# Rotated q and k from SBUF to SBUF by eight transfers of 32 rows, and the transposes of results placed behind the other transposes

## The chip, the core and the metric

The kernel runs on one core of a Trainium2 chip. The metric is the device time of one execution in microseconds (us). Five engines work side by side, each through its own instructions in order: TensorE (PE, with its weight loads as PEld), VectorE (DVE), ScalarE (ACT), GpSimd (POOL) and SyncE (SP), which here issues nearly all DMA transfers. TensorE writes to PSUM alone; the other engines read its results there.

## What is computed

The reference is one block of a network on a sequence of 1024 tokens with 1024 features. The normed input is projected to twelve segments. One branch is an mLSTM in both directions; the other is a differential attention with 8 heads, and the change lies in it. For each head and each of two half heads j (64 features each), q and k are rotated by their positions, and two softmaxes are subtracted:

```python
dq = apply_rope(b_q.reshape(B, S, DA_HEADS, 2, DA_QK_DIM), positions)
dk = apply_rope(b_k.reshape(B, S, DA_HEADS, 2, DA_QK_DIM), positions)
scores = einsum('bqhjd,bkhjd->bhjqk', qb, k) * scale
p = softmax(scores)
att = einsum('bhqk,bkhd->bqhd', p[:, :, 0] - lam * p[:, :, 1], v)
att = rmsnorm(att, da_subln_g) * (1.0 - lambda_init)
y_b = att * silu(b_z)
```

Both branches are gated, projected, summed, added to the input and normed. All of it is float32 outside; inside, TensorE multiplies each float32 operand as a high part and a low part (H and L), in three products.

## The kernel before, in words

The work comes in three stages: projections with the convolution and the gates (to about 410 us of the profile), the attention (410 to 1130 us), and the mLSTM with the three last projections. All instructions of TensorE stand in an order that a planner writes before the build: `Weaver` puts units of work one after another by assumed costs (MM, TP) and assumed delays (the table LAG), and `weave` interleaves two lists, here `main` (the attention's own units) and `nxt` (projections for the next head, and filling work). From the second stage on only TensorE is held to the written order; the order on DVE, ACT and POOL is chosen by the build's scheduler, and each engine then keeps it.

For each of 8 heads h there are 8 tiles of 128 queries, t = 0 to 7. `da_cycle` (L1008 to L1026) lists the units of one cycle (h, t):

- S: `scores`, 12 matmuls S<-kst,qq (L924). They fill two PSUM tiles, one for each half head. Then DVE takes the row maxima (nm, L927, two), ACT the exponentials (e, L929, two), and DVE the reciprocal, a scaling and the difference of both (L933, L934, L935). The result is p of this t.
- T: `transposes`, four transposes of p of t-1 into a PSUM tile (T<-ident,e, L131), two units a cycle. Each tile is then read by ACT (pH, L948) and by DVE (pL, L949).
- PV: `pv`, two units of 12 matmuls (L960), in odd t. They share one PSUM tile, which ACT copies to att (L962).
- M: `squares`, in even t: two transposes of att into a PSUM tile (T<-ident,att, L131), which ACT squares in two steps (L972) and sums for the norm. I call a cycle with M an even cycle.
- G: `scale`, in t = 4 and 5: four transposes of the norm's factors (T<-ident,rb_y) and a DVE multiply (zg, L992).

T, PV, M and G all take their PSUM tile from the tag "T", which has two buffers in turn. So a unit's tile is free when the tile but one before it has been read. In between lie the pieces of the list `nxt`: one piece is an eighth of a projection to 128 features and 512 tokens, three matmuls of 512 columns (pj<-hH,wH and so on, L429), or, for v, six matmuls of 256 columns (L451).

`da_proj` projects q and k of the next head in two halves of 512 tokens. A projection yields its rows in the order (q or k, half head, feature), with both halves of the rotation in two PSUM tiles. `first` and `second` rotate: DVE multiplies (m, L852 and L853, and hl, L863 and L864), POOL combines (m, L865 and L866), ACT rounds to the high part (hl, L868), POOL makes the low part (hl, L869). The tile hl has one buffer. Then `second` has to bring rows from hl to qq and kst, where rotation halves stand below each other. It does so through a DRAM tile stk: four stores (L873) and two loads (L875), all on SP's queue.

Of the kernel before, what the change touches and what calls it, by code (L numbers as in the profile page):

```python
# [7 lines left out]
F32 = mybir.dt.float32  # L8
# [101 lines left out]
class Block:  # L110
# [731 lines left out]
    def da_proj(self, h, st):  # L842
        A, v, a, p, q = self.A, self.v, self.a, self.p, self.q
        w1 = self.w1
        fb = lambda x: x.bitcast(F32)
        kA, kB = ("rope", h, 0), ("rope", h, 1)

        def first(half, pa):
            c = slice(half * 512, (half + 1) * 512)
            m = [w1.tile([128, 512], F32, name=f"m{i}", tag=f"m{i}", bufs=1) for i in range(2)]  # L850
            st["m"] = m
            v.tensor_tensor(out=m[0], in0=pa, in1=self.cosT[:, c], op=ALU.mult)  # L852
            v.tensor_tensor(out=m[1], in0=pa, in1=self.sinT[:, c], op=ALU.mult)  # L853

        def second(half, pb):
            c = slice(half * 512, (half + 1) * 512)
            if half == 0:
                st["k"] = w1.tile([128, 2, S], F32R, name="kst", tag="kst", bufs=2)
            qq = st["q", half] = w1.tile([128, 2, 512], F32R, name="qq", tag="qq", bufs=3)
            m = st["m"]  # L860

            hl = w1.tile([128, 4, 512], F32R, name="hl", tag="hl", bufs=1)
            v.tensor_tensor(out=fb(hl[:, 2]), in0=pb, in1=self.sinT[:, c], op=ALU.mult)  # L863
            v.tensor_tensor(out=fb(hl[:, 3]), in0=pb, in1=self.cosT[:, c], op=ALU.mult)  # L864
            p.tensor_tensor(out=m[0], in0=m[0], in1=fb(hl[:, 2]), op=ALU.subtract)  # L865
            p.tensor_tensor(out=m[1], in0=fb(hl[:, 3]), in1=m[1], op=ALU.add)  # L866
            for i in range(2):
                a.copy(hl[:, i, :], m[i])  # L868
                p.tensor_tensor(out=hl[:, 2 + i, :], in0=m[i], in1=fb(hl[:, i, :]), op=ALU.subtract)  # L869
            dr = self.dram.tile([2, 4, 2, 32, 512], F32, name="stk", tag="stk", bufs=2)  # L870
            for y in range(2):
                for x in range(2):
                    q.dma_start(out=dr[y, :, x], in_=fb(hl[:, 2 * y + x]))  # L873
            for i, x in enumerate((qq, st["k"][:, :, c])):
                q.dma_start(out=fb(x), in_=dr[:, 2 * i:2 * i + 2].rearrange("y j x i s -> (j x i) y s"))  # L875

        kz = ("w_in", OFF["bz"] + 128 * h)

        def zz(half, ps):
            st["g", half] = g = w1.tile([128, 512], F32, name="zg", tag="zg", bufs=2)  # L880
            a.activation(out=g, in_=ps, func=AF.Tanh, scale=0.5)
            v.scalar_tensor_tensor(out=g, in0=g, scalar=1.0, in1=ps, op0=ALU.add, op1=ALU.mult)

        qk = []
        for half in range(2):
            qk += self.proj(kA, half, lambda ps, half=half: first(half, ps))
            qk += self.proj(kB, half, lambda ps, half=half: second(half, ps), name=("qk", h))
        z = self.proj(kz, 0, lambda ps: zz(0, ps)) + self.proj(kz, 1, lambda ps: zz(1, ps), name=("z", h))
        for half in range(2):
            z[(half + 1) * self.PIECES - 1].after = ((("G", h - 1, half), LAG["G"]),)  # L890
        return qk, z
# [114 lines left out]
    @staticmethod  # L1006
    def da_cycle(cur, prev, t):

        before = cur if t > 0 else prev
        un = []  # L1010
        if cur:
            un.append(cur["S"](t))
        own = cur if t >= 4 else prev
        if own and t % 2 == 0:
            un.append(own["M"]((t // 2 - 2) % 4))
        if prev and t in (4, 5):
            un.append(prev["G"](t - 4))
        own = cur if t >= 3 else prev
        pair = ((t - 1) // 2 - 1) % 4
        if own and t % 2 == 1:  # L1020
            un += [own["PV"](pair, 0), own["PV"](pair, 1)]
        if before:
            un.append(before["T"]((t - 1) % 8, 0))
        if before:
            un.append(before["T"]((t - 1) % 8, 1))
        return un  # L1026


# [613 lines left out]
```

## Time and profile before

| | us |
|---|---|
| median of 3 runs | 1722.02 (1720.14 to 1725.31) |
| the profiled execution | 1722.36 |
| its span, first to last instruction | 1720.5 |
| PE busy, PEld busy | 1660.1, 1392.5 |
| DVE, ACT, POOL busy | 988.8, 777.5, 605.6 |
| mean granted TensorE clock | 0.991 |

The span is 1.9 us shorter than the profiled execution's own time; the rest lies around the instructions. PE is busy in 96% of the span, so time is to be had only from its gaps and from stretches at a lower granted clock, and each new gap on PE counts in full. [...]

### The profile page before, as it was taken

What the parts mean: (1) busy time and instruction counts of PE and PEld (TensorE: products, weight loads), DVE (VectorE), ACT (ScalarE), POOL (GpSimd) and SP (SyncE); (2) the same over time, 40 slices, a digit from 0 to 9 for tenths busy, and PEclk for the clock granted to TensorE, in tenths of its full rate; (3) what the DMA queues carried; (4) which work ended last, traced back from release to release, by engine and by line L of the source; (5) the groups of instructions that cost most, each with busy time, mean ns of one, the idle gap of its engine ahead of it and who ended that gap; (6) DMA issues with size and microseconds to landing.
All of it is one profiled execution on the core that took longest, in us unless ns stands there. A gap on an engine that the chain in (4) does not pass through costs nothing. (4 is left out here: it accounts for less than half of the span.)

```text
span 1720.5 us, 25270 instructions
## 1 busy us (share of the span) xinstructions
PE 1660.1 (96%) x9431; PEld 1392.5 (81%) x9431; DVE 988.8 (57%) x1799; ACT 777.5 (45%) x1554; POOL 605.6 (35%) x680
## 2 busy tenths in 40 slices
PE   7999999999999999999999999999999989999998
PEld 5777887887878987798788878889999867888887
DVE  5778678773376665666566655325666643235533
ACT  7455555552355544454445444324655644122221
POOL 4767666664243233323241322222321311222000
PEclk9999999999999999999999999999999999999999
DMA  5343434344322314131422131155455327344222
GB/s 182 94 130 119 137 121 135 111 129 138 113 98 74 111 38 147 62 98 30 131 84 77 45 122 62 62 178 163 139 169 154 96 79 258 123 147 135 86 87 85
DMA packets 182540, 195.55 MB, mean 114 GB/s; under 512 B 10905, under 2 KB 134130, under 8 KB 182418
## 3 DMA queue, kind: packets, MB, share of 16 engines
q1 hardware_dynamic: 181506, 192.35, 35.8%
q8 instruction: 74, 1.21, 0.3%
q10 hardware_dynamic: 912, 1.59, 0.2%
q14 instruction: 48, 0.39, 0.1%
HBM read 130.89 MB, written 63.01 MB: 113 GB/s over the span
## 5 line engine op out<-in xcount | busy, mean ns | idle before, releaser
L429 PE MATMUL pj<-hH,wH 128*128 128x512 f32 x640 | 269.1, 420 | 3.8 <-DVE hl L864 1.9
L429 PE MATMUL pj<-hH,wL 128*128 128x512 f32 x640 | 253.7, 396 | 1.8 <-POOL wL L207 1.8
L429 PE MATMUL pj<-hL,wH 128*128 128x512 f32 x640 | 253.0, 395 | 0.2 <-DVE hL L580 0.2
L209 POOL TENSOR_TENSOR wL<-raw,wH 128x1024 fp32r<-128x1024 f32 x41 | 99.5, 2426 | 287.4 <-ACT wH L204 284.9
L929 ACT ACTIVATE e<-S,nm 128x1024 f32<-128x1024 f32 x128 | 142.5, 1115 | 104.7 <-DVE nm L927 104.6
L927 DVE TENSOR_REDUCE nm<-S 128x1 f32<-128x1024 f32 x128 | 150.4, 1217 | 16.7 <-PE S L924 15.9
L429 PEld LDWEIGHTS pj<-hH,wH 128*128 128x128 f32 x640 | 122.2, 191 | 39.2 <-issue 15.4
L949 DVE TENSOR_TENSOR pL<-T,pH 128x512 fp32r<-128x512 f32 x128 | 87.9, 688 | 108.7 <-ACT pH L948 107.8
L451 PE MATMUL pj<-wH,hH 128*128 128x256 f32 x512 | 149.8, 293 | 0.3
L429 PEld LDWEIGHTS pj<-hH,wL 128*128 128x128 f32 x640 | 121.9, 190 | 30.8 <-POOL wL L207 3.3
L451 PE MATMUL pj<-wL,hH 128*128 128x256 f32 x512 | 144.8, 283 | 1.4 <-POOL wL L207 1.4
L451 PE MATMUL pj<-wH,hL 128*128 128x256 f32 x512 | 144.5, 282 | 0.0
L429 PEld LDWEIGHTS pj<-hL,wH 128*128 128x128 f32 x640 | 122.6, 192 | 18.7 <-DVE hL L580 0.6
L429 PE MATMUL pj<-sl_yb,wH 128*128 128x512 f32 x384 | 121.8, 397 | 4.3 <-ACT sl_yb L1315 2.4
L924 PE MATMUL S<-kst,qq 64*128 64x512 f32 x768 | 108.8, 413 | 8.0 <-DMA kst<-stk 8.0
L948 ACT CAST pH<-T 128x512 fp32r<-128x512 f32 x128 | 74.9, 585 | 88.0 <-PE T L131 87.5
L204 ACT CAST wH<-raw 128x1024 fp32r<-128x1024 f32 x56 | 58.8, 1051 | 114.0 <-PE pj L429 88.3
L451 PEld LDWEIGHTS pj<-wH,hH 128*128 128x128 f32 x512 | 97.8, 191 | 5.1 <-issue 2.2
L451 PEld LDWEIGHTS pj<-wL,hH 128*128 128x128 f32 x512 | 97.5, 190 | 2.3 <-POOL wL L207 2.3
L451 PEld LDWEIGHTS pj<-wH,hL 128*128 128x128 f32 x512 | 97.7, 191 | 0.1
L924 PEld LDWEIGHTS S<-kst,qq 64*128 64x128 f32 x768 | 68.3, 186 | 35.4 <-issue 10.5
L429 PEld LDWEIGHTS pj<-sl_yb,wH 128*128 128x128 f32 x384 | 73.4, 191 | 22.3 <-DVE sl_yb L1316 3.4
(358 smaller groups left out, 4107.0 us busy)
## 6 DMA issues: line engine op xcount, KB each, us to landing
raw<-in_w_in_dram SPq DMA_DIRECT2D x88, 512.0 KB
stk<-hl SPq DMA_DIRECT2D x64, 256.0 KB
qq<-stk SPq DMA_DIRECT2D x16, 512.0 KB
kst<-stk SPq DMA_DIRECT2D x16, 512.0 KB
x<-in_x_dram SPq DMA_DIRECT2D x8, 512.0 KB
cak<-y SPq DMA_DIRECT2D x16, 256.0 KB
cakH<-cin SPq DMA_DIRECT2D x16, 256.0 KB
cakL<-tz SPq DMA_DIRECT2D x16, 256.0 KB
```

The source lines that it names most:

```text
L204: self.a.copy(wH, raw)
L209: self.p.tensor_tensor(out=wL, in0=raw, in1=wHf, op=ALU.subtract)
L429: self.t.matmul(ps, lhsT=l[:, k, :], rhs=r, start=(n == 0), stop=(n == 23))
L451: self.t.matmul(ps[:, i, :], lhsT=l, rhs=r[:, k, :], start=(kh == 0 and k == 0 and m == 0), stop=(kh == 1 and k == 3 and m == 2))
L924: self.t.matmul(ps[:, o], lhsT=qq[r, x, c], rhs=k[r, y, o], start=(m == 0), stop=(m == 2))
L927: v.tensor_reduce(out=nm, in_=ps, axis=AX.X, op=ALU.max, negate=True)
L929: a.activation(out=e, in_=ps, func=AF.Exp, bias=nm[:, 0:1], accum_out=Z[:, j, t:t + 1])
L948: a.copy(pH[:, :, s], ps)
L949: v.tensor_tensor(out=pL[:, :, s], in0=ps, in1=pH[:, :, s].bitcast(F32), op=ALU.subtract)
```

## The change

Two things are changed. The rows go from hl to kst and qq directly, by eight transfers of 32 partitions each (32 rows, high and low part, 512 tokens: 128 KB), with the rotation half x = 0 first. And in `da_cycle` the unit M, which stood right behind S, stands behind both T units.

```diff
-            dr = self.dram.tile([2, 4, 2, 32, 512], F32, name="stk", tag="stk", bufs=2)
-            for y in range(2):
-                for x in range(2):
-                    q.dma_start(out=dr[y, :, x], in_=fb(hl[:, 2 * y + x]))
-            for i, x in enumerate((qq, st["k"][:, :, c])):
-                q.dma_start(out=fb(x), in_=dr[:, 2 * i:2 * i + 2].rearrange("y j x i s -> (j x i) y s"))
+            for x in range(2):
+                for i, to in enumerate((st["k"][:, :, c], qq)):
+                    for j in range(2):
+                        r, g = 64 * j + 32 * x, 64 * (1 - i) + 32 * j
+                        q.dma_start(out=fb(to[r:r + 32]), in_=fb(hl[g:g + 32, x::2]))
...
             un.append(cur["S"](t))
-        own = cur if t >= 4 else prev
-        if own and t % 2 == 0:
-            un.append(own["M"]((t // 2 - 2) % 4))
         if prev and t in (4, 5):
             un.append(prev["G"](t - 4))
...
             un.append(before["T"]((t - 1) % 8, 1))
+        own = cur if t >= 4 else prev
+        if own and t % 2 == 0:
+            un.append(own["M"]((t // 2 - 2) % 4))
         return un
```

The second edit goes through the planner, so the order of PE is the thing to see. This is PE in the cycle of head 2, t = 6, before, from the end of the first three pieces that follow S on. The names: T_6270 is the tile of M, T_6275 and T_6297 are those of the two T units, S_6304 is the next S.

```order
L131 MATMUL T_6270<-ident_146,att_5626 128x128 x2
L131 MATMUL T_6275<-ident_146,e0_6130 128x128 x4
L429 MATMUL pj_6231<-hH0_170,wH_5832 128x512
L429 MATMUL pj_6231<-hL0_172,wH_5832 128x512
L429 MATMUL pj_6231<-hH0_170,wL_5833 128x512
...
L131 MATMUL T_6297<-ident_146,e0_6130 128x128 x4
L924 MATMUL S_6304<-kst_4924,qq_5133 128x512
```

The same place on PE after the change; again three pieces stand between S and the first row. T_6278 and T_6288 are now the tiles of the two T units, T_6301 is that of M.

```order
L131 MATMUL T_6278<-ident_146,e0_6109 128x128 x4
L429 MATMUL pj_6239<-hH0_170,wH_5838 128x512
L429 MATMUL pj_6239<-hL0_172,wH_5838 128x512
L429 MATMUL pj_6239<-hH0_170,wL_5839 128x512
L131 MATMUL T_6288<-ident_146,e0_6109 128x128 x4
...
L131 MATMUL T_6301<-ident_146,att_5632 128x128 x2
...
L923 MATMUL S_6312<-kst_4928,qq_5138 128x512
```

M has moved from the first place to the last: T, one piece, T, two pieces, M, one piece, next S. Of the two buffers, T_6278 has one, T_6288 the other, and M's tile T_6301 takes that of T_6278. Before, it was the second T that took the buffer of M.

DVE after the change, in the same cycle, from the row maxima of this S (S_6243 and S_6244, the two half heads) on:

```order
L926 TENSOR_REDUCE nm_6257<-S_6243 128x1
L926 TENSOR_REDUCE nm_6261<-S_6244 128x1
L932 RECIPROCAL r_6265<-Z_5630 128x1
L933 TENSOR_SCALAR r_6265<-r_6265,Z_5630,nlam_703 128x1
L934 SCALAR_TENSOR_TENSOR e0_6259<-e1_6263,r_6265,e0_6259 128x1024
L948 TENSOR_TENSOR pL_6193<-T_6278,pH_6192 128x4x128
L948 TENSOR_TENSOR pL_6223<-T_6288,pH_6222 128x4x128
```

ACT after the change, in the same cycle:

```order
L928 ACTIVATE e0_6259,Z_5630<-S_6243,nm_6257 128x1024
L928 ACTIVATE e1_6263,Z_5630<-S_6244,nm_6261 128x1024
L947 CAST pH_6192<-T_6278 128x4x128
L947 CAST pH_6222<-T_6288 128x4x128
L971 ACTIVATE T_6301,ms_5631<-T_6301 128x128 x2
```

On DVE and ACT the reads of the two T tiles stand behind the whole softmax of the S that was issued just before them. Before, ACT had the order e0, e1, first square, pH, second square, and DVE had the five softmax rows and then the first pL, as now; but no unit of that cycle waited for that pL.

## Prediction

> **What bounds the kernel now.** I read the page's busy times first:
>
> ```profile
> span 1720.5 us, 25270 instructions
> PE 1660.1 (96%) x9431; PEld 1392.5 (81%) x9431; DVE 988.8 (57%) x1799; ACT 777.5 (45%) x1554; POOL 605.6 (35%) x680
> ```
>
> PE is the bound; DVE and ACT have slack on average. So I asked next what PE waits for in the attention (410 to 1130 us), where the change lies:
>
> ```profile
> PE S L924 <- DMA kst<-stk: 8.0, 3, 2.7
> PE T L131 <- ACT T L972: 5.6, 6, 1.4
> PE pj L429 <- DVE hl L864: 1.9, 1, 1.9
> PE T L131 <- DVE pL L949: 0.3, 1, 0.3
> ```
>
> These four rows (total, times, longest) are all of PE's gaps in the stage, 15.8 us. A wait can cost more than its gap: in four stretches, each beside one of these gaps, the granted clock stood at half. The table by windows (PE busy first, PEclk third from the end):
>
> ```profile
> 428.05:431.46 3.41, 3.41 (x10) 2.64 (x9) 0.00 (x0) 0.51 (x1) 3.41 (x3) 0.50 1.06 383
> 684.05:690.88 6.83, 6.41 (x18) 4.62 (x19) 3.32 (x5) 2.56 (x5) 0.00 (x0) 0.50 0.29 77
> 851.30:854.71 3.41, 3.41 (x8) 2.67 (x9) 2.36 (x2) 2.13 (x3) 0.00 (x0) 0.50 0.47 139
> 1015.14:1018.55 3.41, 3.39 (x10) 2.32 (x11) 1.71 (x2) 0.45 (x1) 0.00 (x0) 0.50 0.57 154
> ```
>
> The hl wait of 1.9 us and the three kst waits (8.0 in three, the longest 2.7) were each followed by this; the ACT waits, up to 1.4 us, were not. A stretch at half costs half of itself: 1.7, 3.4, 1.7 and 1.7, together 8.5 us.
>
> **The change part by part.** *The transfers.* In the second half of head 2, SP's timeline and the S that waited for it read:
>
> ```profile
> 664.66 4.04 SPq L873 DMA_DIRECT2D stk<-hl  x4
> 668.74 2.22 SPq L171 DMA_DIRECT2D raw<-in_w_in_dram  x1
> 679.36 0.37 SPq L875 DMA_DIRECT2D qq<-stk  x1
> 679.78 0.61 SPq L875 DMA_DIRECT2D kst<-stk  x1
> ```
>
> ```profile
> 684.47 1.65 PE L924 MATMUL S<-kst,qq 64*128 64x512 f32 x6 [2.74 <-DMA kst<-stk]
> ```
>
> The stores are issued by 668.70, the loads wait for them until 679.36 (10.7 us), and S goes on at 684.47, 4.7 us after the last load's issue: 15.8 us in two passes. The new way is one pass, and the trace has no such transfer. Bounds: 4.7 us as the loads, 10.7 us as the stores. Both stay under 15.8 - 2.7 = 13.1 us, so the three kst waits go: -8.0 us, and their clock, -6.8 us. I take some 7 us between the ends, and the sum doesn't depend on it. SP issues 128 transfers in place of 96; at the 0.4 to 1.0 us apiece of these rows that is at most 2 us more a half, and in exchange this goes from its queue:
>
> ```profile
> SPq L875 <- DMA stk<-hl: 148.8, 37, 9.2
> ```
>
> Queued behind that wait stand weight loads (raw). No wait of PE on weights stands among its waits in the stage, so their coming earlier is worth nothing. The earlier release of hl removes the 1.9 us wait at 427 us (there DVE could write hl only after the stores had landed) and its half clock, -1.7. Nothing else in the stage waited on these, so nothing is late next on this path.
>
> *M behind the T units.* The six ACT waits of 5.6 us are a second T that waits for the squares of M, whose tile it inherits. That pair is gone: -5.6 us. Removed in all: 8.0 + 5.6 + 1.9 + 8.5 = **24.0 us**.
>
> What replaces it: M now inherits the tile of the first T, and DVE's last read of that tile (pL) stands behind the whole softmax of the S just issued. So I need two times from the start of S: when PE comes to M, and when that pL ends. First PE, from an even cycle without a wait (head 2, t = 2), which has the same pieces in the old order:
>
> ```profile
> 620.32 1.66 PE L924 MATMUL S<-kst,qq 64*128 64x512 f32 x12
> ...
> 624.06 0.38 PE L131 MATMUL T<-ident,att 128*128 128x128 f32 x2
> 624.28 0.60 PE L131 MATMUL T<-ident,e 128*128 128x128 f32 x4
> 624.63 0.48 PE L429 MATMUL pj<-hH,wH 128*128 128x512 f32 x1
> ...
> 627.46 0.60 PE L131 MATMUL T<-ident,e 128*128 128x128 f32 x4
> 627.99 1.65 PE L924 MATMUL S<-kst,qq 64*128 64x512 f32 x12
> ```
>
> S and three pieces take 3.74 us, a T 0.35, four pieces 2.83, which is 0.70 to 0.75 for one and 1.45 for two. The new order (S, three pieces, T, one, T, two, M) brings PE to M at 3.74 + 0.35 + 0.75 + 0.35 + 1.45 = **6.64 us**. Then the softmax after the S at 627.99, on DVE and on ACT (the ACT row at 623.71 belongs to the S at 620.32):
>
> ```profile
> 628.71 0.69 DVE L949 TENSOR_TENSOR pL<-T,pH 128x512 fp32r<-128x512 f32 x1 [0.18 <-ACT pH L948]
> 629.68 2.35 DVE L927 TENSOR_REDUCE nm<-S 128x1 f32<-128x1024 f32 x2 [0.28 <-PE S L924]
> 633.81 1.28 DVE L935 SCALAR_TENSOR_TENSOR e<-e,r,e 128x1024 f32<-128x1024 f32 x1
> ```
>
> ```profile
> 623.71 1.12 ACT L929 ACTIVATE e<-S,nm 128x1024 f32<-128x1024 f32 x1 [1.89 <-DVE nm L927]
> 630.94 1.12 ACT L929 ACTIVATE e<-S,nm 128x1024 f32<-128x1024 f32 x1 [2.26 <-DVE nm L927]
> ```
>
> The first exponential starts 2.95 us after S, the difference ends 4.15 us later (635.09), pL takes 0.69: the tile is free 4.85 us after the first exponential, 7.80 us after S. PE is there at 6.64: a new wait of **1.16 us in an undisturbed even cycle**. At 623.71 the exponential came 3.39 us after S, which makes it 1.60.
>
> A test of this arithmetic on the old order (head 2, t = 6):
>
> ```profile
> 660.71 1.66 PE L924 MATMUL S<-kst,qq 64*128 64x512 f32 x12
> 669.16 0.66 PE L131 MATMUL T<-ident,e 128*128 128x128 f32 x4 [1.12 <-ACT T L972]
> ```
>
> ```profile
> 665.77 1.11 ACT L929 ACTIVATE e<-S,nm 128x1024 f32<-128x1024 f32 x1
> 668.91 0.19 ACT L972 ACTIVATION_READ_ACCUMULATOR T<-T 128x1 f32 x1
> ```
>
> There PE would come to the second T 627.46 - 620.32 = 7.14 us after S, at 667.85; the squares ended at 669.10, and T started at 669.16: 1.3 us late, and the profile shows a gap of 1.12. It also shows why: the exponential came 5.06 us after S, since on ACT the roundings of hl, waiting for POOL, stand ahead of it. That delay repeats wherever a rotation ends just ahead of an even cycle. Three more such places, S on PE and the first exponential on ACT (heads 1, 1, 2; t = 2, 4, 4):
>
> ```profile
> 540.18 1.66 PE L924 MATMUL S<-kst,qq 64*128 64x512 f32 x12
> 560.43 1.66 PE L924 MATMUL S<-kst,qq 64*128 64x512 f32 x12
> 639.71 1.66 PE L924 MATMUL S<-kst,qq 64*128 64x512 f32 x12
> ```
>
> ```profile
> 544.73 1.11 ACT L929 ACTIVATE e<-S,nm 128x1024 f32<-128x1024 f32 x1
> 566.96 1.11 ACT L929 ACTIVATE e<-S,nm 128x1024 f32<-128x1024 f32 x1
> 644.27 1.11 ACT L929 ACTIVATE e<-S,nm 128x1024 f32<-128x1024 f32 x1
> ```
>
> That is 4.55, 6.53 and 4.56 us. The order of ACT, POOL and pieces there is the same after the change, so I keep these delays. In t = 4 a G comes first: with three pieces ahead, arrival at M is 3.74 + 0.35 + 0.75 + 0.35 + 1.45 + 0.35 + 0.75 = 7.74 (odd heads; a v piece has the columns of another piece and is taken alike), with two pieces 7.05. The waits:
>
> - heads 1, 3, 5: t = 0 1.60; t = 2 4.55 + 4.85 - 6.64 = 2.76; t = 4 6.53 + 4.85 - 7.74 = 3.64; t = 6 1.16; together 9.16, times three 27.5.
> - heads 2, 4, 6: 1.60; 1.60; 4.56 + 4.85 - 7.05 = 2.36; 5.06 + 4.85 - 6.64 = 3.27; together 8.83, times three 26.5.
> - head 7, which has no rotation ahead: 1.60, 1.16, 0.75, 1.16, together 4.7. Head 0 has M only in t = 4 and 6, where pL stands ahead of the reciprocal on DVE; taken as 0.
>
> Sum **+58.7 us** of waits. Twelve of them (2.36 to 3.64 us) are longer than the 1.9 us that was followed by a half clock; the bounds for one are nothing and the 3.4 us lost once, and I take 1.7, which three of four showed: **+20.4 us**. Behind M on PE are queued one piece and the next S, and behind that S its softmax; all shift with it, so nothing hides the wait. The squares now come later, but G, their user through POOL, comes two S later (540.18 to 560.43, 20 us). Against the profiled execution: 1722.4 - 24.0 + 58.7 + 20.4 = **1777.5 us**. The median of the runs (1722.0) is the same within 0.4 us.
>
> [...]
>
> **The rivals.** About 0.3% (5 us) is what a measurement of this kernel can tell from no change.
>
> 1. Faster: M finds its tile free. That needs pL to end within 6.64 us of S, so a first exponential within 1.8 us of S; the rows show 2.95 at best, and the order on DVE puts pL behind the softmax. For it: in head 0 pL does stand ahead of the end of the softmax. Then only the gains stay: 1722.4 - 24.0 = **1698 us**.
> 2. The waits come, but the clock stays: 1722.4 - 24.0 + 58.7 = **1757 us**. For it: waits up to 1.4 us left the clock alone, and these come with work on both sides. Against it: four of four gaps from 1.9 us on did not.
> 3. The waits come without the delays, because ACT is earlier there: every first exponential at 2.95. Then per head 1.16, 1.16, 0.06, 1.16 (1, 3, 5) or 1.16, 1.16, 0.75, 1.16 (2, 4, 6, 7), 27.5 us, no half clock: 1722.4 - 24.0 + 27.5 = **1726 us**, no change to speak of. Against it: the delays come from POOL and ACT, which the change leaves as they are.
> 4. The transfers don't do what they say: eight in a row take 13.1 us or more, and the kst waits stay with their clock: 1777.5 + 14.8 = **1792 us**. Against it: both bounds above. [...]
>
> **How the numbers follow.** The forecast, 1777.5 with its own spread of about 1762 to 1790, gets 0.57; rival 1 0.08, rival 2 0.17, rival 3 0.10, rival 4 0.05; 0.03 is left for still more half clock (all twelve at 3.4 us: 1798). The range of 1750 to 1800 leaves out rivals 1 and 3. Faster is rival 1, 0.08. Within 0.3% is most of rival 3, 0.07. Slower is the rest, 0.85.
>
> **What would show it.** Right: a PE wait of M's transposes (T<-ident,att) on DVE pL, some 28 times, near 60 us in all, longest in t = 4 and 6; the waits on kst and on the squares gone; more stretches at half clock between 530 and 1010 us; waits of SP on stk gone. Wrong: no such wait, or the granted clock at 1.00 throughout (rival 2), or waits that are all near 1.2 us (rival 3), or S still waiting for kst (rival 4).

## The result, and the profile after

The changed kernel took 1770.95 us (median of 5 runs, 1766.46 to 1773.43), the kernel before 1721.62 us (median of 5): a ratio of 1.0285, 95% interval 1.0264 to 1.0306. Its profiled execution took 1770.55 us. The page of that execution begins:

```profile
span 1768.7 us, 25390 instructions
PE 1671.1 (94%) x9431; PEld 1394.0 (79%) x9431; DVE 988.3 (56%) x1799; ACT 778.1 (44%) x1554; POOL 603.1 (34%) x680
```

PE has 11 us more of busy time and a smaller share: the 48 us are for the most part idle time. PE's waits in the attention (all between the first and the last S; total, times, longest):

```profile
PE T L131 <- DVE pL L948: 51.0, 30, 3.2
PE T L131 <- ACT att L961: 0.2, 1, 0.2
```

The kst waits and the waits on the squares are gone, as are SP's waits on stk, and one new row stands in their place. The groups by line show that nearly all of it is M's:

```profile
L131 PE MATMUL T<-ident,att 128*128 128x128 f32 x64 | 14.7, 313 | 50.2 <-DVE pL L948 50.2
```

One of these gaps, in head 1, t = 2, on PE, then ACT, then DVE of the same cycle:

```profile
541.34 1.66 PE L923 MATMUL S<-kst,qq 64*128 64x512 f32 x12
...
550.59 0.68 PE L131 MATMUL T<-ident,att 128*128 128x128 f32 x2 [2.38 <-DVE pL L948]
```

```profile
545.29 0.62 ACT L868 CAST hl<-m 128x512 fp32r<-128x512 f32 x1 [0.62 <-POOL m L866]
545.82 1.11 ACT L928 ACTIVATE e<-S,nm 128x1024 f32<-128x1024 f32 x1
```

```profile
548.65 1.28 DVE L934 SCALAR_TENSOR_TENSOR e<-e,r,e 128x1024 f32<-128x1024 f32 x1
549.86 1.28 DVE L948 TENSOR_TENSOR pL<-T,pH 128x512 fp32r<-128x512 f32 x2
```

The first exponential starts 4.48 us after S, behind a rounding of hl that waited for POOL. The combination of the two softmaxes follows on DVE, then two pL of 0.64 us each; the first is over at about 550.5, and M starts at 550.59. The granted clock falls to 0.50 at 550.64. The five stretches at half clock in the attention (PE busy first, PEclk third from the end):

```profile
550.64:554.05 3.41, 3.41 (x13) 2.37 (x15) 0.50 (x1) 0.74 (x4) 1.73 (x3) 0.50 0.60 138
683.76:690.59 6.83, 5.88 (x20) 3.90 (x21) 3.19 (x5) 1.33 (x5) 1.27 (x1) 0.50 0.44 102
755.44:758.85 3.41, 3.41 (x17) 2.85 (x14) 2.69 (x3) 1.17 (x2) 0.00 (x0) 0.50 0.42 127
840.77:844.19 3.42, 3.42 (x15) 2.22 (x14) 0.93 (x1) 0.58 (x4) 0.00 (x0) 0.50 0.66 180
864.66:871.49 6.83, 6.08 (x20) 4.10 (x21) 3.20 (x6) 1.33 (x5) 1.28 (x1) 0.50 0.40 94
```

Where the 48.2 us between the two spans lie (S(0,0) and S(7,7) are the first and the last S; a stretch at half clock counts half; in the first of the five, matmuls of 512 columns start 0.42 us apart, right behind it 0.23):

| stretch | before | after | difference |
|---|---|---|---|
| start to S(0,0) | 457.4 | 455.6 | -1.8 |
| S(0,0) to S(7,7) | 626.1 | 672.4 | +46.3 |
| of that: PE's gaps in the waits | 13.9 | 51.2 | +37.3 |
| of that: half clock, 13.7 and 23.9 us long | 6.8 | 11.9 | +5.1 |
| of that: neither | 605.4 | 609.3 | +3.9 |
| S(7,7) to the end | 637.0 | 640.7 | +3.7 |

The last row is half clock as well: 14.6 us of it stand there before and 22.1 after (in both, 2.1 us of the last stretch lie behind the last instruction), which makes 3.7 us, in a part of the program that the change leaves alone.

### The profile page after: what moved, and what is told of

The parts are those of the page before. It is cut to its first block, busy times and chain, and to the rows that moved or that the text cites. A ratio compares the mean times of both kernels' runs of the same rounds, so it can differ in the third digit from the quotient of the medians.

```text
span 1768.7 us, 25390 instructions
## 1 busy us (share of the span) xinstructions
PE 1671.1 (94%) x9431; PEld 1394.0 (79%) x9431; DVE 988.3 (56%) x1799; ACT 778.1 (44%) x1554; POOL 603.1 (34%) x680
```

## The experiments

The theory: M inherits the tile of the first T, and that tile's last read (pL) comes late, behind the softmax on DVE and behind exponentials that are late themselves. The rivals: the transfers of 32 rows cost; the late place of M costs as such; DVE's combination alone is to blame. Each run was timed beside the kernel before on the same chip, and the ratio is to that.

**The transfers alone.** The changed kernel with M put back behind S:

```
             un.append(cur["S"](t))
+        own = cur if t >= 4 else prev
+        if own and t % 2 == 0:
+            un.append(own["M"]((t // 2 - 2) % 4))
...
             un.append(before["T"]((t - 1) % 8, 1))
-        own = cur if t >= 4 else prev
-        if own and t % 2 == 0:
-            un.append(own["M"]((t // 2 - 2) % 4))
```

> The eight transfers, with the squares' transposes back in front of the other transposes of the even cycle. Theory (the changed kernel is slower because the squares' transposes inherit the tile of the first T and wait for its low part behind the softmax): that wait is gone, the gains of the transfers stay, 8.0 (kst) + about 1 (hl) + some 8.5 us of half clock, while the 5.6 us of waits on the squares stay as in the kernel before: 1704 us, between 1700 and 1712. Rival (the transfers of 32 rows are what costs): 1722 us or more, with S waiting for kst or qq.

1707.32 us, ratio 0.9913 (0.9898 to 0.9928). The waits of the attention:

```profile
PE T L131 <- ACT T L971: 5.6, 6, 1.4
PE T L131 <- DVE pL L948: 0.3, 1, 0.3
```

No S waits for kst or qq, and there is no half clock between the first and the last S (the mean granted clock of the profiled execution was 0.995, the changed kernel's 0.988). The transfers are a gain of 15 us; the loss lies in the other half of the change.

**The move alone**, with the way through DRAM: the kernel before, with M's three lines behind the T units.

> The squares' transposes moved behind the others, with the rotated q and k still going through DRAM. Theory: about 50 us in some 30 gaps of PE on DVE pL as in the changed kernel, and the kst waits back in part, since the waits give the transfers time: 1780 us, between 1768 and 1790. Rival (the transfers cost): the move saves its 5.6 us, 1716 us.

1773.06 us, ratio 1.0296 (1.0281 to 1.0312). Between the first and the last S:

```profile
PE T L131 <- DVE pL L949: 50.6, 30, 3.2
...
PE S L924 <- DMA kst<-stk: 0.2, 1, 0.2
```

The move makes all of the loss, +51 us. And 7.8 of the 8.0 us of kst waits have gone without the new transfers: PE comes later to each S, and the loads through DRAM are in time. So behind a late M the transfers are worth some 2 us (1773.06 to 1770.95), not 15, and the intervals of the two ratios (1.0281 to 1.0312 and 1.0264 to 1.0306) overlap, so that it could be nothing.

**The softmax cut short**, in the changed kernel:

```
-            r = w1.tile([128, 1], F32, name="r", tag="r", bufs=1)
-            v.reciprocal(out=r, in_=Z[:, 1, t:t + 1])
-            v.tensor_scalar(out=r, in0=r, scalar1=Z[:, 0, t:t + 1], scalar2=self.nlam[:, 0:1], op0=ALU.mult, op1=ALU.mult)
-            v.scalar_tensor_tensor(out=e0, in0=e, scalar=r[:, 0:1], in1=e0, op0=ALU.mult, op1=ALU.add)
```

> The changed kernel without the combination of the two softmaxes: reciprocal, r and the 128x1024 scalar_tensor_tensor on DVE are left out, so e0 alone is transposed; PE, ACT and SP keep their order. Theory: pL of the first T then stands on DVE behind the two maxima only, some 4.2 us after S, and ends before PE comes to the squares (6.64 us after S): the 51.0 us of gaps and the 12 us of half clock go, 1707 us, between 1700 and 1715. Rival (the late place of the squares costs by itself, through ACT or a later PV): no less than 1755 us.

1728.76 us, ratio 1.0037 (1.0024 to 1.0049): 42 of the 64 us that were expected. A third of the gaps stayed:

```profile
PE T L131 <- DVE pL L944: 17.2, 16, 2.0
```

The theory was incomplete. The same place as above shows what it lacked, ACT first:

```profile
542.55 0.62 ACT L868 CAST hl<-m 128x512 fp32r<-128x512 f32 x1 [0.63 <-POOL m L866]
543.08 1.11 ACT L928 ACTIVATE e<-S,nm 128x1024 f32<-128x1024 f32 x1
...
545.27 1.06 ACT L943 CAST pH<-T 128x512 fp32r<-128x512 f32 x2
```

```profile
545.88 1.29 DVE L944 TENSOR_TENSOR pL<-T,pH 128x512 fp32r<-128x512 f32 x2 [3.12 <-ACT pH L943]
```

DVE now stands idle for 3.12 us until pH is there, and pH stands on ACT behind both exponentials. So the tile is held on two engines; without the combination it is free some 3.5 us after the first exponential, and not 4.8. Where a rounding of hl holds up that exponential, this is still too late.

**The control for it**: the same work left out of the transfers alone.

> Control for the shortened softmax (1728.8 us with the squares behind, 17.2 us of gaps left of 51.0): the same work left out (reciprocal, r, the combination of e0 and e1) with the transfers and the squares in front. Theory: in that order nothing on PE waits for the combination, so leaving it out is worth nothing: 1707 us as with it (1707.3), between 1703 and 1711, squares' waits 5.6 us as before. Rival (DVE work left out shortens the cycle anywhere): 1697 us or less.

1706.53 us, ratio 0.9906 (0.9888 to 0.9924); squares' waits 5.5 us. With M in front, nothing waits for the combination. So the 42 us were not DVE work saved but waits for M's tile (51.0 to 17.2 us, 33.8 less) and half clock behind them (11.9 to 3.4 us, 8.5 less).

**The roundings on POOL**, in the changed kernel:

```
-                a.copy(hl[:, i, :], m[i])
+                p.tensor_copy(hl[:, i, :], m[i])
```

> The changed kernel with the two roundings of hl on POOL instead of ACT, so that no exponential stands on ACT behind a rounding that waits for POOL. Theory (the tile is free 4.8 us after the first exponential, and the long waits come from exponentials that the roundings hold up): every first exponential some 2.9 to 3.4 us after S, waits of 0.8 to 1.4 us in every even cycle, about 24 us in place of 51.0, and no half clock from them: 1732 us, between 1722 and 1742. Rival (the waits come from the combination on DVE alone): waits stay near 50 us and 1765 us or more.

1737.85 us, ratio 1.0091 (1.0076 to 1.0106). The waits, and head 1, t = 2 on PE and ACT:

```profile
PE T L131 <- DVE pL L948: 29.7, 25, 2.0
```

```profile
540.01 0.50 PE L923 MATMUL S<-kst,qq 64*128 64x512 f32 x2
...
548.16 0.44 PE L131 MATMUL T<-ident,att 128*128 128x128 f32 x2 [1.27 <-DVE pL L948]
```

```profile
543.09 1.12 ACT L928 ACTIVATE e<-S,nm 128x1024 f32<-128x1024 f32 x1 [3.08 <-DVE nm L926]
```

The exponential comes 3.08 us after S, in place of 4.48, and M's gap is 1.27 us, in place of 2.38. All long gaps but one of 2.0 us are under 1.5 us, and no half clock is left in the attention (mean granted clock 0.996). That is 33 us of the 49, so the combination alone is not to blame either.

**Both taken away**: the roundings on POOL, and the combination left out.

> The changed kernel with both delays of its pL taken away: the roundings of hl on POOL, and the combination of the two softmaxes (reciprocal, r, scalar_tensor_tensor) left out. Theory: the first exponential comes at 2.9 to 3.4 us, the tile is free 3.5 us later (as in the run with the short softmax), at 6.4 to 6.9 us, about when PE comes to the squares (6.6 to 7): fewer than ten gaps, under 3 us in all, no half clock, 1705 us, between 1698 and 1710. Rival (the late place of the squares has a price of its own besides the tile): 1715 us or more.

1705.26 us, ratio 0.9903 (0.9884 to 0.9921). The waits between 430 and 1110 us:

```profile
PE T L131 <- DVE pL L944: 1.5, 7, 0.3
```

M stands where it stood in the changed kernel, and the 49 us are gone. The run is 5 us above the best one below, which has M in front; the gaps make 1.5 us of these, which leaves some 3 us for the late place as such and for all else in which the two runs differ.

**M with a tile of another kind**, one line of the changed kernel:

```
         def squares(t2):
-            pt = self.bank("T")
+            pt = self.psA.tile([128, 512], F32, name="pj", tag="pj", bufs=2)
```

> The changed kernel with one edit: the squares' tile comes from the two PSUM buffers of the projections (pj) instead of those of T; every engine keeps its order. Theory (the wait is for the tile of the first T): the 30 gaps on pL at the squares go; in their place a projection that opens after the squares may wait until the one before it is read, 0 to 3 us in up to four places of a head: between 1700 and 1745 us, 1715 taken. Rival (it is not the tile: the squares wait there whatever tile they take): gaps of the squares' transposes near 50 us, 1765 us or more.

1706.60 us, ratio 0.9914 (0.9899 to 0.9930). M's row in the groups by line, and the waits between 430 and 1110 us:

```profile
L131 PE MATMUL pj<-ident,att 128*128 128x128 f32 x64 | 12.2, 272 | 0.0
```

```profile
PE pj L429 <- ACT gt L837: 2.3, 2, 1.7
PE T L131 <- DVE pL L948: 0.8, 1, 0.8
PE T L131 <- ACT att L961: 0.2, 1, 0.2
PE pj L429 <- ACT pj L971: 0.2, 1, 0.2
```

The order of every engine is that of the changed kernel, and the softmax and the roundings are as late as there. With another tile M waits for nothing, as its row says (the last number is its idle time). The projections that were to pay for it wait 2.5 us in all. Without their gaps (2.8 and 5.9 us), this run and the one with the transfers alone take 606.9 and 605.3 us from the first S to the last, so the late place as such makes less than 2 us. This settles the cause: it is the tile, and next to nothing of it is the place.

**M between the two T units.**

> The changed kernel with the squares' transposes between the two T of the even cycle. Theory (the third unit of an even cycle inherits the first one's tile, whatever it is): no wait at the squares, but the second T now waits for pL of the first; it comes some 0.6 us later than the squares did (about 7.2 us after S), so 30 gaps of together about 34 us, and 1750 us, between 1742 and 1762. Rival (it is the squares that are slow to start): the wait goes with them or vanishes, under 1715 us.

1720.08 us, ratio 0.9991 (0.9980 to 1.0002); the forecast of 1750 was wrong. The second T waits, as said, but less:

```profile
PE T L131 <- DVE pL L948: 8.6, 4, 2.6
PE T L131 <- ACT T L971: 6.8, 9, 1.5
```

I had taken it that the third unit of a cycle always gets the first one's buffer. In nine of its waits the second T waited for the squares: it had M's tile. (One of the four waits on pL, 0.8 us in head 0, is a first T's.) So the pool doesn't always hand its two buffers out in turn, as I had written of the kernel before: in the program of this run the second T has M's tile in 25 of the 31 cycles with T, M, T.

**The same with the roundings on POOL.**

> Squares between the two T (1720.1 us, 15.7 us of gaps of the second T), with the roundings of hl on POOL. Theory: those gaps come from late exponentials, both where the second T took the squares' tile (6.8 us) and where it took the first T's (8.6 us): they shrink to under 6 us, 1709 us, between 1702 and 1714. Rival (the place in the middle costs by itself): 1716 us or more.

1701.97 us, ratio 0.9884 (0.9866 to 0.9902), just under what was expected. PE waits for nothing between 430 and 1110 us, so both kinds of wait came from late exponentials.

**Twice as many transfers.** The transfers alone, each of the eight cut into two of half the columns:

```
-                        q.dma_start(out=fb(to[r:r + 32]), in_=fb(hl[g:g + 32, x::2]))
+                        for s in (slice(0, 256), slice(256, 512)):
+                            q.dma_start(out=fb(to[r:r + 32, :, s]), in_=fb(hl[g:g + 32, x::2, s]))
```

> The transfers alone (squares in front, 1707.3 us), with each of the eight transfers cut into two of half the columns: sixteen issues per half. Theory (the transfers have slack ahead of S): the last lands some 5 us later, at 12 to 13 us behind hl, near the 13 us of the way through DRAM, so S waits for kst or qq 0 to 8 us in all: 1707 to 1720 us. Rival (each transfer of 32 rows costs the path something): 1722 us or more.

1707.93 us, ratio 0.9920 (0.9905 to 0.9935). SP's timeline for the first half of head 0, and the landing of one transfer (KB, median us):

```profile
413.58 2.68 SPq L875 DMA_DIRECT2D kst<-hl  x4
416.36 2.51 SPq L875 DMA_DIRECT2D qq<-hl  x4
418.97 2.50 SPq L875 DMA_DIRECT2D kst<-hl  x4
421.52 2.51 SPq L875 DMA_DIRECT2D qq<-hl  x4
```

```profile
kst<-hl SPq DMA_DIRECT2D x128, 64.0 KB, 2.1
```

Their issue takes 10.4 us in place of 5.4, and no S waits. The transfers have at least 5 us of slack.

**A version that beats both.** The transfers alone with the roundings on POOL:

> The transfers alone (1707.3 us) with the roundings of hl on POOL: theory: the six waits of the second T on the squares (5.6 us in all) come from the same late exponentials and go: 1702 us, between 1698 and 1705. Rival (POOL is late then, and S waits for kst and qq, or PE for the next pieces): 1707 us or more.

1700.46 us, ratio 0.9874 (0.9859 to 0.9889). All PE waits from 405 to 1190 us, and the window that holds the attention from its first S on:

```profile
PE pj L429 <- DVE zg L881: 1.4, 1, 1.4
PE T L127 <- ACT kwH L1081: 1.0, 1, 1.0
PE pj L451 <- DVE vL L1035: 0.6, 1, 0.6
```

```profile
455.00:1059.00 604.00, 603.98 (x3842) 501.84 (x3841) 402.76 (x546) 295.78 (x615) 223.21 (x213) 1.00 0.24 64
```

PE is busy for 603.98 of 604.00 us at full clock: by the profile, nothing but PE's own work is left in this stage.

## Why the prediction was right, and where it was off

The forecast was 1777.5 us, the result 1770.95. Part of that closeness is luck. Of the +55.1 us that were forecast, 48.2 came between the two spans: the half clock of the attention was forecast 8.5 us too high and the waits 3.9, while the stretch ahead of S(0,0) gained 1.8 us less than forecast and 3.7 us came behind the attention, where nothing was forecast.

**The new waits: right, in place, cause and size.** M waits in every even cycle of heads 1 to 7, 28 times. The forecast counted 58.7 us from start to start; the gaps, which begin when the last matmul ahead has ended, make 51.0. Gap by gap, t = 0, 2, 4, 6: in head 1 1.43, 2.38, 3.07 and 0.82 us (forecast 1.60, 2.76, 3.64, 1.16), in head 2 1.31, 1.35, 1.95 and 2.96 (1.60, 1.60, 2.36, 3.27). Between the first and the last S the gaps and the 3.9 us that are neither gap nor half clock come to +41.2 us; the forecast less the kst and the squares' waits (58.7 - 13.6) is +45.1. A gap doesn't hold the whole wait: most even cycles with one are longer than the same cycle of the run with another tile by the gap and some 0.2 us more. The forecast's test on the old order, that late exponentials are what makes a squares' wait, was right as well: with the roundings on POOL those six waits are gone too.

**"DVE's last read of that tile (pL) stands behind the whole softmax": right, but half of the cause.** The short softmax showed pH behind both exponentials on ACT as well. It changed no number, since the 4.85 us were read off a cycle that had both.

**The half clock: the term that was mis-sized.** I took 1.7 us for each of twelve long waits, 20.4 us. Five were followed by half clock, 11.9 us, and seven of up to 3.2 us were not. The step that failed is "longer than the 1.9 us that was followed by a half clock": the length of a gap doesn't decide. In the changed kernel the stretches begin at 550.64, 683.76, 755.44, 840.77 and 864.66 us, 39, 21, 25 and 7 times 3.413 us apart. Counted in windows of 3.413 us from these starts on, as far as these traces show, what decides is how much idle time falls into one window: ahead of the five stretches it was 2.38, 2.00, 1.79, 1.94 and 2.19 us. The gap of 3.07 us at head 1, t = 4 stands in the changed kernel across a boundary (busy time of PE is the second number, PEclk third from the end):

```profile
571.12:574.53 3.41, 1.96 (x17) 1.75 (x15) 0.75 (x3) 3.41 (x7) 2.18 (x2) 1.00 0.41 99
574.53:577.95 3.42, 1.80 (x14) 1.25 (x14) 2.16 (x3) 0.84 (x5) 0.00 (x0) 1.00 0.86 199
577.95:581.36 3.41, 3.41 (x29) 3.25 (x28) 3.14 (x4) 2.23 (x4) 0.00 (x0) 1.00 0.37 115
```

It left PE idle for 1.45 and 1.62 us of two windows, and the clock stayed. In the run of the move alone the same gap, 3.07 us too, fell differently:

```profile
573.66:577.07 3.41, 1.17 (x11) 0.96 (x8) 1.55 (x3) 2.72 (x6) 1.40 (x2) 1.00 0.22 58
577.07:583.90 6.83, 6.00 (x26) 4.65 (x26) 3.79 (x6) 1.58 (x6) 0.00 (x0) 0.50 0.40 130
```

One window has 2.24 us of idle time, and half clock follows. The same twelve gaps led to seven stretches in that run, which cost 17.1 us, and to five here, 11.9: the size of this term hangs on where the gaps fall.

**The removed waits: the sum held, the shares did not.** I booked 8.0 us of kst waits and 6.8 us of their half clock to the transfers. Either part of the change takes the kst waits away by itself: with the transfers alone none is left, with the move alone 0.2 us. The total counted them once and didn't suffer. But the two parts by themselves, -15 and +51 us, add up to 36, and together they make 49.

**"Nothing is late next on this path": not quite.** In place of the hl wait of 1.9 us PE waits there 1.4 us for zg, as in the last run above. The half clock that followed at 428 us is gone, as forecast.

**The transfers: right.** In the first half of head 0:

```profile
413.77 1.40 SPq L874 DMA_DIRECT2D kst<-hl  x2
415.27 1.23 SPq L874 DMA_DIRECT2D qq<-hl  x2
416.60 1.23 SPq L874 DMA_DIRECT2D kst<-hl  x2
417.88 1.24 SPq L874 DMA_DIRECT2D qq<-hl  x2
```

```profile
kst<-hl SPq DMA_DIRECT2D x64, 128.0 KB, 2.4
```

The last of the eight is issued by 419.1 and lands some 2 us later, about 7 us after the first issue, as I took between 4.7 and 10.7. The first row here is the changed kernel while the eight of a half run, the second the run with sixteen transfers of half the size (GB/s at the end):

```profile
432.00:437.50 5.50, 5.50 (x46) 5.41 (x45) 0.69 (x1) 1.63 (x3) 3.14 (x3) 1.00 0.77 179
415.00:425.00 10.00, 10.00 (x46) 8.18 (x44) 0.79 (x2) 1.32 (x2) 4.78 (x2) 1.00 0.42 104
```

That is 179 and 104 GB/s. SP issues a transfer every 0.64 to 0.75 us in both, and half the size goes at 0.58 of the rate, so I put these rates down to the pace of the issue; no run here shows such transfers at a faster pace. It costs nothing here, since S has no use for the data so early. Rival 4 falls by both runs on the transfers, and so do the other three: rival 1 (no wait) and rival 3 (no late exponentials) by the gaps, rival 2 (the clock stays) by the five stretches.

**Outside the forecast** are the 3.7 us of half clock behind the attention. The other runs have between 14.6 and 22.1 us of it there, with the order of the work unchanged. For one of these stretches, at 1458.58 us in the changed kernel, the traces before and after show what may set it. Ahead of it PE runs two groups of eight transposes (T<-ident,hm), with a gap of 0.53 us ahead of the first and one of 0.50 us ahead of the second, in both traces alike. In the changed kernel the first gap begins at 1455.48, 0.31 us into a window, and half clock follows; in the kernel before it begins at 1409.32, 1.65 us into one, and none does. So it looks like a shift against the windows. For the rest of the 3.7 us this isn't shown.

## What to carry to other kernels

When a unit of work is moved in a rotation of buffers, ask whose buffer it gets and behind what that buffer's last reader is queued, on every engine that reads it; PE's order alone looks harmless. Don't add up what the parts of a change save before asking whether one part's wait hides the other's: here the transfers were worth 15 us alone and some 2 us, no more than the noise, beside the move. If the place is wanted, another tile is the cheaper cure: one line gave back 64 us.

## What the runs showed of the hardware

Half clock came in steps of 3.413 us: in the traces before and after all its stretches begin whole numbers of 3.413 us apart (before, counted from the one at 428.05: 75, 124, 172, 279, 300 and 378; after, from 550.64: 39, 60, 85, 92, 256, 266, 278 and 356), and all but the last of each trace are 3.41 or 6.83 us long. In windows of that length, between 405 and 1190 us, the nine stretches of the two traces followed windows with 1.79 to 2.57 us of PE idle time. All seven windows at full clock with 1.94 us or more were followed by one, and none with 1.68 us or less; in between, those with 1.79 and 1.88 us were, and one with 1.89 us was not. In a window that was itself at half, less was enough: where it had 0.43 to 1.07 us of idle time a second one at half followed (six times, three of them behind the attention), and where it had 0.02 us or less full clock came back. That is the difference between stretches of 6.83 and of 3.41 us. Further on, in the changed kernel, the stretch at 1458.58 us followed a window of only 1.24 us, while after 1.54 us (the window at 1212.82) and, in the kernel before, 1.80 us (at 1353.06) the clock stayed, so idle time isn't the whole of it; in the window of 1.24 us PE ran eight transposes over 1.97 us, all but 0.22 us of it shown as busy, while four of the attention's take 0.60. The idle times are worked out from PE's rows, whose ends are modelled, so the bound is not sharper than that. With the roundings on POOL 25 gaps came one after the other between the first and the last S, 29.7 us in all and the longest 2.0, and none did it.

On ACT the two roundings of hl, 0.62 us each, waited for POOL (in head 1 2.71 and 0.62 us in t = 2, 3.76 and 0.63 in t = 4) and the first exponential came behind them, 4.48 and 6.48 us after S. With the roundings on POOL it came 3.08 us after S in t = 2, 1.40 us earlier. Giving them to POOL, which was then busy for 633.2 us in place of 603.1, was worth 33 us in the changed kernel and 7 us in the other order.
